# Two of eight weighted one-hots made by GpSimd, eight U blocks fewer ahead of the expert loop, and later loads of G: a hybrid encoder layer on one core

## The chip, the cores and the metric

The kernel runs on one core of a Trainium2 chip. The metric is the device time of one execution in microseconds (us). Three runs of the kernel before gave 1571.31, 1573.11 and 1576.31; their median is 1573.11 us. The profile is of one further execution. The core has a matrix engine (TensorE, PE in the profile; PEld are its weight loads), VectorE (DVE), ScalarE (ACT), GpSimd (POOL) and SyncE (SP), each with a queue of its own that it works off in order, and 16 DMA engines that all queues share.

## The reference

One encoder layer over 512 tokens of width 1024, all in float32: a layer norm; a projection; neighbourhood attention and latent attention; an output projection; a layer norm; then the expert layer (PEER) with a gated embedding term; a last layer norm. The change touches only the expert layer:

```python
q = (xb @ w_q).reshape(128, 8, 256)                       # 8 heads
s1, s2 = q[..., :128] @ sub_keys[0].T, q[..., 128:] @ sub_keys[1].T
v1, i1 = top_k(s1, 16);  v2, i2 = top_k(s2, 16)
cv, ci = top_k(all 256 sums v1 + v2, 16)                  # 16 experts a head
e1, e2 = i1[ci // 16], i2[ci % 16]                        # expert number = 128 * e1 + e2
g = softmax(cv)
hpre = einsum('td,ted->te', xb, u_table[128 * e1 + e2])   # 16384 rows of U, V
out  = einsum('te,ted->td', g * gelu(hpre), v_table[128 * e1 + e2])
```

Each token so uses 128 of 16384 rows of U and as many of V, with the weights g.

## The kernel before

**Two ways to reach the rows.** The tokens stand in four chunks of 128. For chunk 0 the kernel fetches each token's rows of U and V by indirect DMA from GpSimd (gathers). For the other 384 tokens it goes through all 128 blocks of 128 experts: for each block it multiplies with the block's V and weights that are zero where a token did not pick an expert. These weights are G (block by block, from DRAM) times the activation `ge` = gelu(U x). For 96 of the 384 tokens (the "own rows", `own_rows`, L1025) the products with U are also made from gathered rows, and only 288 tokens (N_U) go through U blocks.

**Ahead of the loop.** Under a schedule written out by hand, five strands run together:

- `route` (L863), on VectorE: the top 16 and the picks of one chunk.
- `build_g` (L956): makes G for one chunk in 16 passes of eight tokens (OT). A pass makes eight one-hots of e1 (`oh_i`: the first few by one VectorE operation at L997, the rest by ScalarE at L1001 and L1002) and eight one-hots of e2, weighted with g (`oh_j`: eight VectorE operations at L1010). TensorE multiplies them pairwise (`products`, L976), ScalarE copies the result out (L987), and every second pass ScalarE's queue writes 1 MB of G to DRAM (L989). The tiles have two buffers, so a pass takes the buffers of the pass before the last one.
- `own_rows`: 96 gathers of 512 KB by GpSimd (L1045) into four buffers (`whi`, `wlo`), each used by one VectorE operation (L1047).
- The gate's products (L104 to L106) and their cuts.
- U blocks ahead (`lead_block`, L1082): LEAD = 73 blocks are loaded (L1067, three buffers) and multiplied uncut in float32 (L1092), eight products each; the result is activated by ScalarE (L1074). The first SPILL = 56 results go to DRAM (L1076) and are read back in the loop (L1371); the rest stay in SBUF, in LEAD - SPILL + 1 buffers.

What TensorE does between two VectorE steps is set by a planner: each strand yields the VectorE time that it has issued, `run_pe` (L947) adds it times PACE to `due`, and takes U products and gate products off their list until `due` is used up. `run` (L1196) does the same for the own rows with a share (OWN = 0.98): for each microsecond of other VectorE work it issues that share of own-row work. The order of the builds is: route chunk 1, then route and build chunks 2 and 3 among the own rows, route chunk 0, and last build chunk 1 (L1236 to L1239), with five of eight `oh_i` from VectorE instead of two.

**The passage.** After the last build GpSimd's queue holds seven gathers for chunk 0 (L1276), the first load of G (L1250, in two parts), and further gathers; the last U blocks ahead, the first loads of V and the first blocks' cuts come beside them (L1323 to L1341).

**The loop** (L1345) takes one block of V a step. VectorE multiplies G with `ge` (L1376), ScalarE and VectorE cut V and the weights into two parts of float32r (`split`, L86), TensorE makes 18 products of 512 columns into six sums (`acc`, `mm3`). As long as blocks of U are left (n + 1 + LEAD < 128), the step also makes one of them (`expert_in`, L770): a load, a cut and 24 products of 288 columns. The gathers of chunk 0 (L1276, L1291) and their VectorE operations (L1282, L1293) are spread over the steps, half as many in steps without a U block (LATE). G is loaded for eight steps at a time into two buffers, in the middle of the group before (L1348), from SP's queue; V's loads (L1260) and the read back `ge` stand in the same queue.

Of the kernel before, what the change touches and what calls it, by code (L numbers as in the profile page):

```python
# [15 lines left out]
OP = mybir.AluOpType  # L16
# [17 lines left out]
N_U = N_D - N_S  # L34
GT = 16
GB = 8
LEAD = 73
SPILL = 56
FIRST = 8
PACE = 1.1  # L40
AHEAD = 14.0
LAG = 6.0
PRE = 14
OWN = 0.98
OWN_LATE = 10.0
LATE = 0.5
OT = 8
OV = 5
OV_OWN = 2
NEG = -1e30  # L50
# [15 lines left out]
def tile_encoder_layer(ctx: ExitStack, tc: tile.TileContext, A: dict, out: bass.AP):  # L66
    nc = tc.nc
# [689 lines left out]
    NGC, NDC = N_G // 128, N_D // 128  # L757
# [32 lines left out]
    iota = rt.tile([128, 128], F32, name="iota")  # L790
# [41 lines left out]
    first = []  # L832
# [120 lines left out]
        if due < -1e6:  # L953
            due = 0.0

    def build_g(c, e1, e2, gw, first):  # L956


        nonlocal due
        ps = ps_tile("tr")  # L960
        for i, x in enumerate((e1, e2, gw)):
            nc.tensor.transpose(ps[:, i * 128:(i + 1) * 128], x, ident)
        due -= 0.35
        yield None
        eT = bt.tile([128, 3, 128], F32, name="eT")
        nc.vector.tensor_copy(eT, ps[:, 0:384].rearrange("p (a b) -> p a b", b=128))
        yield 0.6
        ne = bt.tile([128, 128], F32, name="ne")
        nc.scalar.mul(ne, ps[:, 0:128], -1.0)

        def products(q, oi, oj):
            out = []
            for r in range(OT // 4):
                ps = ps_tile("tr")
                for i in range(4):
                    nc.tensor.matmul(ps[:, i * 128:(i + 1) * 128], oj[:, 4 * r + i, :], oi[:, 4 * r + i, :],  # L976
                                     start=True, stop=True)
                out.append(ps)
            return out

        def leave(q, sums):
            nonlocal stage
            if q * OT % GT == 0:
                stage = bt.tile([128, 128, GT], F32, name="g_st")
            for r, ps in enumerate(sums):
                x = OT * q % GT + 4 * r
                nc.scalar.copy(stage[:, :, x:x + 4], ps.rearrange("p (t i) -> p i t", t=4))  # L987
            if (q + 1) * OT % GT == 0:
                nc.scalar.dma_start(g_dram[(c - NGC) * (128 // GT) + q * OT // GT], stage.rearrange("p i t -> p (i t)"))  # L989

        stage = None
        ahead = None
        for q in range(128 // OT):
            t0 = OT * q

            oi = bt.tile([128, OT, 128], F32, name="oh_i")
            nc.vector.tensor_tensor(oi[:, 0:first], iota.unsqueeze(1).to_broadcast([128, first, 128]),  # L997
                                    eT[:, 0, t0:t0 + first].unsqueeze(2).to_broadcast([128, first, 128]),
                                    op=OP.is_equal)
            for i in range(first, OT):  # L1000
                nc.scalar.activation(oi[:, i], iota, AF.Abs, bias=ne[:, t0 + i:t0 + i + 1])  # L1001
            nc.scalar.activation(oi[:, first:OT], oi[:, first:OT], AF.Relu, bias=1.0, scale=-1.0)  # L1002
            if ahead:
                sums = products(*ahead)
                due -= 1.8
            yield 0.15 * first

            oj = bt.tile([128, OT, 128], F32, name="oh_j")
            for i in range(OT):
                nc.vector.tensor_scalar(oj[:, i], iota, eT[:, 1, t0 + i:t0 + i + 1], eT[:, 2, t0 + i:t0 + i + 1],  # L1010
                                        op0=OP.is_equal, op1=OP.mult)
                if i == OT // 2 - 1:
                    yield 0.257 * OT / 2
            if ahead:
                leave(ahead[0], sums)
            ahead = (q, oi, oj)
            yield 0.257 * OT / 2
        sums = products(*ahead)
        due -= 1.8
        yield 0.3  # L1020
        leave(ahead[0], sums)
# [60 lines left out]
    def lead_block():  # L1082


        while len(raws) < 3 and loaded < LEAD:
            load_u()
# [109 lines left out]
    def run(steps, share=0.0, n=2):  # L1196

        nonlocal own_due
        for amount in steps:
            if amount is None:  # L1200
                for _ in range(n if own else 0):
                    run_pe(next(own, 0.0))
                continue
            run_pe(amount)
            own_due += amount * share
            while own and own_due > 0:
                x = next(own, None)
                if x is None or not x:
                    own_due = -1e9
                    break  # L1210
                run_pe(x)
                own_due -= x

    with tc.manual_schedule(engines={nc.vector.engine, nc.scalar.engine, nc.tensor.engine, nc.sync.engine,
                                     nc.gpsimd.engine}):
        for _ in range(3):
            load_u()
        held = []
        run(route(NGC, held))
        own = own_rows(*held)  # L1220
        run_pe(next(own))
        own_due = -OWN_LATE
        for c in range(NGC + 1, 4):
            res = []
            run(route(c, res), OWN)
            run(build_g(c, *res, OV_OWN), OWN)
        lead0 = route(0, [])
        for _ in range(14):
            run([next(lead0)], OWN)
        own_due = 1e9  # L1230
        run([0.0], 1.0)
        for _ in own:
            pass
        own = None
        run_pe(LAG)
        build = build_g(NGC, *held, OV)  # L1236
        next(build)
        run(lead0)
        run(build)  # L1239
        pb.close()  # L1240
# [82 lines left out]
    with tc.manual_schedule(engines={nc.vector.engine, nc.scalar.engine, nc.tensor.engine, nc.sync.engine,  # L1323
# [3 lines left out]
        gt_next = load_g(0, nc.gpsimd, ((128 // GT, NTG), (0, 128 // GT)))  # L1327
# [15 lines left out]
    with tc.manual_schedule(engines={nc.vector.engine, nc.sync.engine}):  # L1343
        expert_in(LEAD)
        for n, i in enumerate(order):  # L1345
            if n % GB == 0:
                gt = gt_next
            if n % GB == GB // 2 and n + GB // 2 < 128:  # L1348
                gt_next = load_g(n + GB // 2)
            raw = v_next[n] if n < 3 else load_v(n)  # L1350
            if n in v_cut:
                vh, vl = v_cut[n]
                ah = pP.tile([128, N_D], F32R, name="a_hi")
                al = pP.tile([128, N_D], F32R, name="a_lo")
            elif n in (124, 125):
                vh = wst.tile([128, D], F32R, name="whi")
                vl = wst.tile([128, D], F32R, name="wlo")
                a2 = wst.tile([128, 2, N_D], F32R, name="raw", bufs=3)
                ah, al = a2[:, 0], a2[:, 1]
            else:  # L1360
                if in_wst(n):
                    vh = wst.tile([128, D], F32R, name="whi")
                    vl = wst.tile([128, D], F32R, name="wlo")
                else:
                    vh = pP.tile([128, D], F32R, name="v_hi")
                    vl = pP.tile([128, D], F32R, name="v_lo")
                ah = pP.tile([128, N_D], F32R, name="a_hi")
                al = pP.tile([128, N_D], F32R, name="a_lo")
            if 0 <= n + GE_AHEAD - (128 - SPILL) < SPILL:
                ge = pB.tile([128, N_U], F32, name="ge", bufs=LEAD - SPILL + 1)  # L1370
                nc.sync.dma_start(ge, ge_dram[order[n + GE_AHEAD]])  # L1371
                ge_t[order[n + GE_AHEAD]] = ge
            ge = ge_t.pop(i)
            a = gt[:, :, n % GB, :]
            dn = gt[:, N_S // GT:, n % GB, :]
            nc.vector.tensor_tensor(dn, dn, ge.rearrange("p (g t) -> p g t", t=GT), op=OP.mult)  # L1376
            if n not in v_cut:
                split(vh, vl, raw)
            split(ah.rearrange("p (g t) -> p g t", t=GT), al.rearrange("p (g t) -> p g t", t=GT), a)
            late.append((n, ah, al, vh, vl))  # L1380
            if n < 124:
                for c in range(NDC):
                    expert_out(late[0], c)
                late = []
            if n + 1 + LEAD < 128:
                expert_in(n + 1 + LEAD)
            if n >= NO_GATHER:
                spent += 1 if n + LEAD < 128 else LATE
            upto = min(len(steps), PRE + math.ceil((len(steps) - PRE) * spent / (128 - (1 - LATE) * LEAD - 3 - NO_GATHER)))
            for f in steps[done:upto]:  # L1390
                f()
            done = upto
        for c in range(NDC):
            for hf in range(2):
                for x in late:
                    expert_out(x, c, (hf,))
# [101 lines left out]
```

## Time and profile before

| | us |
|---|---|
| median of three runs | 1573.11 |
| the profiled execution | 1577.96 |
| its span, first to last instruction | 1576.2 |
| TensorE busy in the span | 1536.5 |
| VectorE busy | 1311.2 |
| ScalarE busy | 691.5 |
| GpSimd busy | 490.2 |
| granted TensorE clock, mean | 0.994 |

The busy time of an engine is the time in which at least one of its instructions runs. TensorE's records overlap, so what one product costs is read from the distance of two starts, as the chain of waits gives it. A line number can be that of a helper: L104 to L106 are the products of every cut matrix, L89 and L90 every cut. A row of the chain is: start, length, engine, tile, line, count. A row of the timeline is: start, length, engine, line, operation, tiles, shapes, count, and in brackets the idle time before it and what ended it. A row by tile or line is: shortest, median and longest duration in ns, first and last start.

### The profile page before, as it was taken

To read this page: it belongs to the slowest core of one execution; us is meant where nothing else is said; L and a number is where in the kernel's file an instruction comes from. 1 tells how busy PE (TensorE), PEld (TensorE's weight loads), DVE (VectorE), ACT (ScalarE), POOL (GpSimd) and SP (SyncE) were. 2 spreads that over 40 slices of the span, in tenths; PEclk is the share of its full clock that TensorE was granted. 3 is DMA by queue.
4 is the path that set the end of the run, shared out by engine and by line. 5 is a ranking of instruction groups with operands and counts; after the bars stand their busy time and mean duration, and the time that the engine had idled before them with its cause. 6 is when DMAs were issued, how large, how long until landed. Compare 5 with 4: busy or idle time off the path is not lost.

```text
span 1576.2 us, 23358 instructions
## 1 busy us (share of the span) xinstructions
PE 1536.5 (97%) x7963; PEld 1277.3 (81%) x7963; DVE 1311.2 (83%) x2989; ACT 691.5 (44%) x1269; POOL 490.2 (31%) x496
## 2 busy tenths in 40 slices
PE   9999999999999999999998999999999999999997
PEld 5788777788878887878786889889899888787885
DVE  7376785679899999789894899889889889799997
ACT  3365675333224672565562343434444333333333
POOL 1013110010024233432104455545555534344410
PEclk9999999999999999999999999999999999999999
DMA  6333230152369999999669999999999999999972
GB/s 224 97 112 95 76 121 28 52 153 81 106 211 347 348 377 346 362 381 373 237 237 387 376 383 378 387 376 349 376 374 338 363 368 381 387 372 387 384 285 80
DMA packets 204571, 437.21 MB, mean 277 GB/s; under 512 B 16770, under 2 KB 110370, under 8 KB 201380
## 3 DMA queue, kind: packets, MB, share of 16 engines
q1 hardware_dynamic: 138592, 210.27, 38.6%
q0 software_dynamic: 53984, 191.97, 32.7%
q10 hardware_dynamic: 11876, 33.49, 5.5%
q8 instruction: 63, 1.03, 0.3%
q14 instruction: 56, 0.46, 0.1%
HBM read 394.54 MB, written 37.62 MB: 274 GB/s over the span
## 4 chain that ended last, share of the span: by engine, by line
PE 76%; DVE 9%; DMA 7%; issue 5%; POOL 2%; ACT 1%; SPq 0%; POOLq 0%; DVEq 0%; ACTq 0%
PE acc L104 10%; PE acc L106 10%; PE acc L105 10%; PE mm L1092 5%; PE tr L976 4%; PE hp L104 4%; PE hp L105 4%; PE hp L106 4%; PE pj L104 3%; PE mm L104 3%; PE pj L105 3%; PE pj L106 3%; PE mm L106 3%; PE mm L105 3%; PE hp L1092 2%
## 5 line engine op out<-in xcount | busy, mean ns | idle before, releaser
L1291 POOL DMA_INDIRECT gat<-in_v_rows_dram,i_sel x128 | 169.6, 1325 | 204.0 <-DVE base L1293 179.4
L1276 POOL DMA_INDIRECT gat<-in_u_rows_dram,i_sel x128 | 168.9, 1320 | 181.4 <-DVE scr L1282 124.4
L104 PE MATMUL acc<-v_hi,a_hi 128*128 128x512 f32 x552 | 216.3, 392 | 3.8 <-ACT a_hi L89 3.8
L106 PE MATMUL acc<-v_hi,a_lo 128*128 128x512 f32 x552 | 216.5, 393 | 0.0
L105 PE MATMUL acc<-v_lo,a_hi 128*128 128x512 f32 x552 | 215.6, 391 | 0.0
L90 DVE TENSOR_TENSOR wlo<-raw,whi 128x1024 fp32r<-128x1024 f32 (+3 forms) x134 | 157.0, 1172 | 67.4 <-ACT whi L89 56.0
L89 ACT CAST whi<-raw 128x1024 fp32r<-128x1024 f32 (+3 forms) x134 | 135.1, 1009 | 140.0 <-PE mm L105 40.4
L89 ACT CAST v_hi<-v_raw 128x1024 fp32r<-128x1024 f32 x92 | 96.6, 1050 | 203.0 <-issue 126.7
L1293 DVE SCALAR_TENSOR_TENSOR base<-gat,hdot,base 128x1024 f32<-128x1024 f32 x128 | 163.9, 1280 | 1.7
L1282 DVE SCALAR_TENSOR_TENSOR scr<-gat,h 128x1024 f32<-128x1024 f32 x128 | 156.6, 1223 | 2.9
L1092 PE MATMUL mm<-whole,raw 128*128 128x288 f32 x624 | 157.7, 406 | 0.5 <-ACT ge L1074 0.4
L1092 PE MATMUL hp<-whole,raw 128*128 128x288 f32 x544 | 138.8, 410 | 5.3 <-DMA raw<-in_uT_dram 5.3
L89 ACT CAST a_hi<-gt 128x384 fp32r<-128x384 f32 x126 | 64.6, 513 | 180.3 <-DVE gt L1376 122.1
L1092 PEld LDWEIGHTS mm<-whole,raw 128*128 128x128 f32 x624 | 115.8, 190 | 30.7 <-issue 1.3
L90 DVE TENSOR_TENSOR v_lo<-v_raw,v_hi 128x1024 fp32r<-128x1024 f32 x92 | 112.6, 1223 | 24.1 <-issue 12.0
L1092 PEld LDWEIGHTS hp<-whole,raw 128*128 128x128 f32 x544 | 103.3, 192 | 33.6 <-issue 4.2
L104 PE MATMUL hp<-hTh,whi 128*128 128x288 f32 x440 | 130.2, 296 | 0.0
L106 PE MATMUL hp<-hTh,wlo 128*128 128x288 f32 x440 | 129.9, 295 | 0.0
L105 PE MATMUL hp<-hTl,whi 128*128 128x288 f32 x440 | 129.8, 295 | 0.0
L104 PEld LDWEIGHTS acc<-v_hi,a_hi 128*128 128x128 f32 x552 | 104.0, 189 | 24.6 <-ACT a_hi L89 4.4
L106 PEld LDWEIGHTS acc<-v_hi,a_lo 128*128 128x128 f32 x552 | 103.8, 188 | 23.6 <-DVE a_lo L90 0.9
L105 PEld LDWEIGHTS acc<-v_lo,a_hi 128*128 128x128 f32 x552 | 104.1, 189 | 20.8 <-issue 0.2
(375 smaller groups left out, 3383.7 us busy)
## 6 DMA issues: line engine op xcount, KB each, us to landing
raw<-in_uT_dram SPq DMA_DIRECT2D x128, 512.0 KB
v_raw<-in_v_rows_dram SPq DMA_DIRECT2D x94, 512.0 KB
g_dram<-g_st ACTq DMA_DIRECT2D x24, 1024.0 KB
gt<-g_dram SPq DMA_DIRECT2D x15, 1536.0 KB
raw<-in_v_rows_dram SPq DMA_DIRECT2D x34, 512.0 KB
raw<-in_w_in_dram SPq DMA_DIRECT2D x16, 512.0 KB
raw<-in_w_q_dram SPq DMA_DIRECT2D x16, 512.0 KB
ge_dram<-ge ACTq DMA_DIRECT2D x56, 144.0 KB
```

The costliest lines, as they stand in the source:

```text
L89: nc.scalar.copy(hi, src)
L90: nc.vector.tensor_tensor(lo, src, r32(hi), op=OP.subtract)
L104: nc.tensor.matmul(ps, a[0], b[0], start=start, stop=False)
L105: nc.tensor.matmul(ps, a[0], b[1], start=False, stop=False)
L106: nc.tensor.matmul(ps, a[1], b[0], start=False, stop=stop)
L976: nc.tensor.matmul(ps[:, i * 128:(i + 1) * 128], oj[:, 4 * r + i, :], oi[:, 4 * r + i, :], start=True, stop=True)
L1092: nc.tensor.matmul(ps[:, :N_U], raw[:, k], whole[:, k, :], start=(k == 0), stop=(k == 7))
L1276: nc.gpsimd.indirect_dma_start(out=u[:], out_offset=None, in_=u_rows, in_offset=bass.IndirectOffsetOnAxis(ap=i_sel[:, c, k:k + 1], axis=0))
L1282: nc.vector.scalar_tensor_tensor(scr, u, 1.0, h[c], op0=OP.mult, op1=OP.mult, accum_out=hdot[:, c, k:k + 1])
L1291: nc.gpsimd.indirect_dma_start(out=u[:], out_offset=None, in_=v_rows, in_offset=bass.IndirectOffsetOnAxis(ap=i_sel[:, c, k:k + 1], axis=0))
L1293: nc.vector.scalar_tensor_tensor(base[c], u, hdot[:, c, k:k + 1], base[c], op0=OP.mult, op1=OP.add)
```

## The change

In a build, the last `pooled` of a pass's eight `oh_j` are made by GpSimd instead of VectorE, with the same operation: two in chunks 2 and 3, four in the last build (chunk 1). They are issued ahead of VectorE's. The planner's costs follow VectorE's smaller share, and the own rows' share in the builds becomes 1.25 (OWN_B), so that each pass keeps its two own rows. LEAD becomes 65 and SPILL 48: eight blocks of U less ahead of the loop, eight more in it, eight results less written and read back; 17 stay in SBUF as before. In the loop, a group of G that is loaded at a step without a U block is loaded at the group's seventh step instead of its fifth, so two loads of V come ahead of it in SP's queue.

```diff
-LEAD = 73
-SPILL = 56
+LEAD = 65
+SPILL = 48
...
+OWN_B = 1.25
...
+OP_OWN = 2
+OP_LAST = 4
...
-    def build_g(c, e1, e2, gw, first):
+    def build_g(c, e1, e2, gw, first, pooled):
...
-            for i in range(OT):
-                nc.vector.tensor_scalar(oj[:, i], iota, eT[:, 1, t0 + i:t0 + i + 1], eT[:, 2, t0 + i:t0 + i + 1],
-                                        op0=OP.is_equal, op1=OP.mult)
-                if i == OT // 2 - 1:
-                    yield 0.257 * OT / 2
+            mine = OT - pooled
+            for i in list(range(mine, OT)) + list(range(mine)):
+                engine = nc.vector if i < mine else nc.gpsimd
+                engine.tensor_scalar(oj[:, i], iota, eT[:, 1, t0 + i:t0 + i + 1], eT[:, 2, t0 + i:t0 + i + 1],
+                                     op0=OP.is_equal, op1=OP.mult)
+                if i == mine // 2 - 1:
+                    yield 0.257 * (mine // 2)
...
-            yield 0.257 * OT / 2
+            yield 0.257 * (mine - mine // 2)
...
-            run(build_g(c, *res, OV_OWN), OWN)
+            run(build_g(c, *res, OV_OWN, OP_OWN), OWN_B)
...
-        build = build_g(NGC, *held, OV)
+        build = build_g(NGC, *held, OV, OP_LAST)
...
-            if n % GB == GB // 2 and n + GB // 2 < 128:
-                gt_next = load_g(n + GB // 2)
+            if n % GB == (GB // 2 if n < 128 - LEAD + 4 else GB - 2) and n // GB < 128 // GB - 1:
+                gt_next = load_g(n // GB * GB + GB)
```

## The prediction

> **What bounds the kernel now.** First the page: its span, TensorE's share, and the DMA rate slice by slice.
>
> ```profile
> span 1576.2 us, 23358 instructions
> PE 1536.5 (97%) x7963; PEld 1277.3 (81%) x7963; DVE 1311.2 (83%) x2989; ACT 691.5 (44%) x1269; POOL 490.2 (31%) x496
> ...
> GB/s 224 97 112 95 76 121 28 52 153 81 106 211 347 348 377 346 362 381 373 237 237 387 376 383 378 387 376 349 376 374 338 363 368 381 387 372 387 384 285 80
> ...
> raw<-in_uT_dram SPq DMA_DIRECT2D x128, 512.0 KB
> ...
> ge_dram<-ge ACTq DMA_DIRECT2D x56, 144.0 KB
> ```
>
> A share over the whole span hides which wait ends last, so next the busy time of each engine by stage (columns: PE, PEld, DVE, ACT, POOL busy with counts, clock, DMA share, GB/s). The stages: build of chunk 2, build of chunk 3, the last build (chunk 1), the passage to the loop, the loop's steps with a U block, its steps without.
>
> ```profile
> 491.70:590.50 98.80, 98.16 (x539) 82.83 (x538) 91.27 (x235) 71.44 (x169) 31.54 (x33) 1.00 0.99 365
> 646.20:736.00 89.80, 87.03 (x487) 72.92 (x486) 76.57 (x210) 65.07 (x159) 31.00 (x33) 1.00 0.99 380
> 766.30:823.00 56.70, 54.12 (x359) 47.91 (x359) 51.56 (x154) 41.95 (x104) 5.86 (x7) 1.00 0.70 260
> 823.00:857.60 34.60, 27.32 (x114) 20.95 (x112) 13.12 (x21) 7.39 (x12) 15.85 (x15) 0.95 0.98 362
> 857.60:1261.00 403.40, 401.63 (x2286) 359.95 (x2287) 361.01 (x490) 158.25 (x220) 212.27 (x154) 1.00 1.00 371
> 1261.00:1566.30 305.30, 303.83 (x1315) 245.65 (x1314) 267.75 (x341) 109.65 (x151) 105.95 (x84) 1.00 0.92 337
> ...
> 491.70:743.90 252.20, 248.29 (x1291) 204.82 (x1290) 226.16 (x618) 148.82 (x352) 84.22 (x84) 1.00 0.99 369
> ```
>
> The loop is TensorE alone: 401.6 of 403.4 us and 303.8 of 305.3. The two builds that hold the own rows (all gathers of `own_rows` are used by 743.9) are full on two sides: TensorE at 97 to 99% and the DMA engines at 0.99. VectorE stands at 85 to 92%. In the last build the DMA engines have room (0.70).
>
> Third, the chain of waits, for what one piece of TensorE work takes: a U block ahead of the loop (16 records), a pass's eight products, a U block inside the loop (24 rows from 869.50 to 872.70), and a step's output products (18 rows from there).
>
> ```profile
> 549.46 3.88 PE hp L1092 x16
> 553.35 1.78 PE tr L976 x16
> ...
> 869.50 0.14 PE hp L104
> ...
> 872.57 0.13 PE hp L106
> 872.70 0.23 PE acc L104
> ...
> 876.59 0.23 PE acc L106
> ```
>
> So a U block costs 3.88 us ahead and 3.20 us in the loop.
>
> **The change part by part.** *Eight U blocks move from ahead of the loop into it.* The activation of each block in the loop dates the steps:
>
> ```profile
> L777 ACT ACTIVATE ge<-hp x55: 395/404/408, 860.0 to 1260.6; 128x288 f32<-128x288 f32 x55
> ```
>
> 54 steps in 400.6 us are 7.42 us a step; the 74 steps after it take 305.3, 4.13 each. Eight steps change from 4.13 to 7.42: +26 us. Bounds: 8 x 3.20 = 25.6 and 8 x 3.29 = 26.3; TensorE hides nothing here, because it is the bound. Each block also brings one more split; VectorE has room (361 of 403). DMA: 8 x 0.52 MB more U, less 8 x 0.15 MB of `ge` read back, on 403.4 x 371 + 305.3 x 337 = 253 MB that now have 26 us longer: covered. The gathers stay the same in number, spread thinner.
>
> Ahead of the loop the same blocks free 8 x 3.88 = 31 us of TensorE. If all of that left the time, the change would win 5 us. The question is what is late next, and it differs by stage. By the order of the two programs, 2.2 of the eight are gone by the start of chunk 3's build and 4.6 by the start of the last one; own rows keep their places, two a pass (so the new share 1.25 costs nothing: it only makes up for shorter passes).
>
> *Own part, 491.7 to 743.9.* TensorE loses 4.6 x 3.88 = 18 us, VectorE 64 one-hots. Their price, and a pass of the last build:
>
> ```profile
> 783.98 0.82 DVE L997 TENSOR_TENSOR oh_i<-iota,eT 128x640 f32<-128x640 f32 x1
> 784.72 2.15 DVE L1010 TENSOR_SCALAR oh_j<-iota,eT 128x128 f32<-128x128 f32 x8
> 786.77 0.83 DVE L997 TENSOR_TENSOR oh_i<-iota,eT 128x640 f32<-128x640 f32 x1
> ```
>
> Eight in 2.15, 0.27 us each: 64 are 17 us. But DMA loses only 4.6 x 0.67 = 3.1 MB of 252.2 x 369 = 93 MB: 8.4 us at the same rate. At the best slice's 387 GB/s the remaining 90 MB would take 233 us, 20 less; that is the other end. What speaks against it is GpSimd's queue. It runs in order, and now two one-hots stand behind every two gathers. A one-hot of pass q waits for the products of pass q-2, whose buffer it takes; the gathers behind it wait too, and VectorE waits for those. How long a gather takes, and that VectorE already waits:
>
> ```profile
> 682.83 10.18 DMA whi<-in_u_rows_dram,s_sel
> ```
>
> ```profile
> DVE whi L1047 <- DMA whi<-in_u_rows_dram,s_sel: 14.0, 10, 2.1
> ```
>
> ```profile
> 676.63 1.22 DVE L1047 SCALAR_TENSOR_TENSOR whi<-whi,h_s 128x1024 f32<-128x1024 f32 x1 [1.28 <-DMA whi<-in_u_rows_dram,s_sel]
> ...
> 677.78 0.42 DVE L997 TENSOR_TENSOR oh_i<-iota,eT 128x256 f32<-128x256 f32 x1
> 678.12 1.11 DVE L1010 TENSOR_SCALAR oh_j<-iota,eT 128x128 f32<-128x128 f32 x4
> ```
>
> A pass is 89.8/16 = 5.6 us. Counted from the start of pass q-1, the products of q-2 end at about 1.8, two one-hots at 2.4, and the gather is out at 3.3; VectorE wants it at 5.6 + 2.3 (own row 1.15, `oh_i` 0.34, three `oh_j` 0.8). That leaves 4.6 us. Before, a gather went out when the own row four places earlier was used: four half passes of 2.8, less 1.2 for that row and 1.2 for the issue, left about 9, and landing took 10.2 with four in flight. With two in flight, 4.6 us at 380 GB/s move 1.75 MB, and the gather with the other traffic's share (0.52 + 0.89) fits just so. So the queue eats between 0 and some 0.5 us a pass (16 us in 32 passes). The own part comes out between -20 and +8; I take -4, half the fall that the bytes allow, because both ends need one of two full resources to give.
>
> *Last build.* VectorE loses 4 x 0.27 a pass, and of U's products between the passes 51 become 27 in the order, so TensorE loses 24/8 x 3.88 = 12 us of 57. Before, the products of 13 passes stand between these rows, 12 intervals of 3.08 us:
>
> ```profile
> 778.81 1.78 PE tr L976 x16
> ...
> 815.77 1.78 PE tr L976 x16
> ```
>
> ```profile
> 780.00:820.00 40.00, 40.00 (x273) 36.12 (x272) 37.84 (x119) 31.93 (x79) 0.00 (x0) 1.00 0.62 232
> ```
>
> ScalarE is next: 31.9 of 40 us, 2.46 a pass. GpSimd's one-hot does not stand in the trace; its nearest rows:
>
> ```profile
> 313.00 0.23 POOL L789 IOTA iota_i<- 128x128 int32 x1 [88.68 <-PE mm L105]
> ...
> 316.67 6.19 POOL L813 TENSOR_TENSOR whole<-hTh,hTl 128x288 f32<-128x288 f32 x8 [1.77 <-DVE hTl L90]
> ```
>
> Between 0.23 (writes 128 columns, reads none) and 6.19/8 = 0.77 (reads two inputs of 288). I take 0.3, near the row of the same length. Four are 1.2 us, hidden behind ScalarE; at 0.77 they are 3.1 and nothing is won. So 0 to -10 us over 16 passes; I take -6.
> The Trainium skill's "GPSIMD Engine Reference", section "Elementwise — side-by-side cycle accounting", gives 1.03 cycles an element for a body of at most two operations; by that a one-hot would be an estimated 0.11 us and a dispatch, and the sum would be the same.
>
> *Passage to the loop.* Today GpSimd issues seven gathers in the last build's free DMA time, then stands waiting for G:
>
> ```profile
> 765.55 0.94 POOL L1276 DMA_INDIRECT gat<-in_u_rows_dram,i_sel  x1 [30.82 <-DVE gws L1053]
> ...
> 773.04 0.94 POOL L1276 DMA_INDIRECT gat<-in_u_rows_dram,i_sel  x1 [0.30 <-issue]
> 823.48 1.25 POOL L1250 DMA_DIRECT2D gt<-g_dram  x1 [49.50 <-PE tr L976]
> ```
>
> Now 64 one-hots stand ahead of them, so 7 x 0.52 = 3.7 MB come some 40 us later, into the stage where TensorE waits for U twice:
>
> ```profile
> 829.27 13.11 DMA raw<-in_uT_dram
> ...
> 848.35 7.43 DMA raw<-in_uT_dram
> ```
>
> At 387 GB/s that is 9.5 us if the cover is gone and 0 if it all fits before the last product; I take +4.
>
> *G's late loads.* The load waits on SP for VectorE's last use of the buffer; V's loads wait behind it.
>
> ```profile
> SPq L1250 <- DVE a_lo L90: 44.7, 7, 7.2
> ```
>
> Two V loads pass ahead of it now; G itself still goes out when its buffer comes free, eight steps ahead. TensorE idles 1.5 us in that stage, so at most that: -1.
>
> Sum: -4 -6 +4 = -6 ahead of the loop, +26 -1 in it: **+19 us**. The profiled execution took 1577.96 (span and 1.8 around it), 4.9 over the median 1573.11; laid on the median, **1592 us**.
>
> **The rivals.** *TensorE alone paces everything (faster).* Its 97 to 99% in the builds speak for it: then all 31 us leave, +26 -2 come back, -7: 1566. Against it: the own part would have to shrink by 18 us at a DMA rate that the trace shows only in its best slices, and the passage must not grow. It decides from 26 us saved ahead of the loop.
> *DMA gives its best rate (a little slower or equal).* Own part -20, the rest as above: -22 + 25 = +3, 1576. For it: the loop holds 371 GB/s over 400 us.
> *GpSimd's queue starves the own rows.* Half a microsecond to one a pass, 16 to 32 us over -8: lead +6 to +22, net +31 to +47, 1604 to 1620. For it: the 4.6 us above; against: fewer gathers in flight land sooner.
> *The one-hots only change place.* Both engines lengthen beside each other:
>
> ```profile
> L1010 DVE TENSOR_SCALAR oh_j<-iota,eT x384: 327/343/559, 494.8 to 816.9; 128x128 f32<-128x128 f32 x192
> ```
>
> ```profile
> L1045 POOL DMA_INDIRECT whi<-in_u_rows_dram,s_sel x48: 939/944/1687, 453.9 to 731.3; - x48
> ```
>
> If they excluded each other, a pass of the last build would be 0.74 + 4 x 0.27 + 4 x 0.3 = 3.0 us, nothing won: +25, 1598; at 0.77 it is 4.9, +29 more: 1627.
> The Trainium skill's "SBUF — State Buffer", section "Who interferes with whom", says just this: a VectorE operation in a two-port mode, or with two SBUF inputs, and a reading GpSimd operation block each other whole. The maxima above agree with it; no run yet shows two such streams.
>
> **How the numbers follow.** Forecast (1585 to 1604) 0.46; TensorE alone 0.18; DMA at its best 0.16; GpSimd's queue 0.15; excluded one-hots beyond 1604 0.05. A measurement here can tell about 0.3%, 4.7 us: faster is below 1568.4, the first rival, 0.18; same takes 0.12 of the DMA rival; slower is the rest, 0.70. The range reaches from 1565, the first rival's time, to 1612, the middle of the queue rival's; some 0.15 lies outside.
>
> **What would show it.** Right: loop steps of 7.4 us, 63 of them; TensorE idle in the builds with DMA still at 0.97 or more; the last build's passes at 2.5 to 2.8 us with ScalarE full; gathers of `gat` issued after the last one-hot. Wrong: the builds at over 385 GB/s and TensorE full (then faster); VectorE's waits for the `whi` rows well above 14.0 us, GpSimd idle before its one-hots (then slower); one-hots over 0.6 us on GpSimd, or `oh_j` on VectorE over 0.4 in the mean.

## The result, and the profile after

The changed kernel takes 1658.33 us, the median of four runs from 1653.32 to 1662.07, beside 1572.21 us for the kernel before: a ratio of 1.0525, 95% interval 1.0488 to 1.0561 (the ratios in this document are not exactly the quotients of the medians). So it is slower, and by some 86 us instead of the 19 that were forecast. The profiled execution took 1662.07 us.

First the stages, in the columns of the prediction's table (busy time of PE, PEld, DVE, ACT, POOL with counts, clock, DMA share, GB/s): build of chunk 2, build of chunk 3, last build, passage, loop with U blocks, loop without; then the part with the own rows as a whole.

```profile
492.10:613.00 120.90, 101.74 (x517) 84.33 (x516) 82.89 (x199) 70.21 (x166) 78.26 (x67) 0.90 0.80 286
672.90:779.90 107.00, 85.51 (x442) 72.12 (x441) 69.56 (x177) 64.78 (x156) 75.94 (x66) 0.89 0.83 297
814.60:881.20 66.60, 52.98 (x311) 42.39 (x311) 30.16 (x81) 40.98 (x99) 64.85 (x68) 1.00 0.37 150
881.20:923.00 41.80, 26.60 (x108) 20.37 (x108) 18.98 (x29) 7.06 (x12) 19.06 (x19) 0.84 1.02 382
923.00:1384.00 461.00, 461.00 (x2638) 414.04 (x2637) 405.66 (x538) 182.07 (x255) 237.29 (x168) 1.00 0.99 365
1384.00:1650.60 266.60, 266.60 (x1158) 216.53 (x1156) 234.80 (x304) 95.23 (x132) 85.89 (x69) 1.00 0.90 326
```

```profile
492.10:792.40 300.30, 253.75 (x1225) 207.99 (x1224) 213.19 (x554) 148.05 (x347) 173.36 (x149) 0.91 0.84 301
```

The own part, from the first copy of `eT` to the end of the last own row, went from 252.2 to 300.3 us (+48.1), the last build from 56.7 to 66.6 (+9.9), the passage from 34.6 to 41.8 (+7.2), the loop from 708.9 to 727.6 (+18.7). With 0.2 us elsewhere that is the 84.1 us between the two spans, 1576.2 and 1660.3. (The prediction's row for the build of chunk 2 ends at 590.5, 4 us before that build's last product; like for like, its 98.8 us are 103.1, beside 120.9 now.) In the own part nothing is full any more: TensorE fell from 98% to 84%, DMA from 0.99 to 0.84, VectorE from 90% to 71%, GpSimd stands at 58%. No resource is the bound by itself; they wait for each other in turn. The granted TensorE clock, 1.00 before, is 0.91 here; what that costs, no run shows by itself. In the last build one engine is full, and it is GpSimd: 64.85 of 66.60.

Next, who waits, from 480 to 900 us (engine, line, waited for; sum, times, longest).

```profile
DVE wlo L1052 <- DMA wlo<-in_u_rows_dram,s_sel: 53.9, 23, 6.1
POOL oh_j L1015 <- PE tr L979: 49.1, 16, 16.5
...
DVE whi L1052 <- DMA whi<-in_u_rows_dram,s_sel: 30.1, 15, 4.4
PE tr L979 <- DVE oh_j L1015: 29.6, 13, 5.2
```

The same view of the kernel before has for the other pair of buffers:

```profile
DVE wlo L1047 <- DMA wlo<-in_u_rows_dram,s_sel: 6.7, 7, 1.6
```

VectorE's waits for the own rows were 14.0 and 6.7 us and are 30.1 and 53.9. GpSimd waits 49.1 us for products before its one-hots, and TensorE waits for VectorE's one-hots. What a one-hot takes, in ns (shortest, median, longest):

```profile
L1015 DVE TENSOR_SCALAR oh_j<-iota,eT x256: 331/342/684, 495.4 to 874.4; 128x128 f32<-128x128 f32 x128
L1015 POOL TENSOR_SCALAR oh_j<-iota,eT x128: 783/835/2436, 492.7 to 876.1; 128x128 f32<-128x128 f32 x128
```

On VectorE it costs what it did; on GpSimd never less than 783 ns, where the prediction took 300.

### The profile page after: what moved, and what is told of

Read it like the earlier page. It is cut to its first block, busy times and chain, and to the rows that moved or that the text cites. A ratio compares the mean times of both kernels' runs of the same rounds, so it can differ in the third digit from the quotient of the medians.

```text
span 1660.3 us, 23579 instructions
## 1 busy us (share of the span) xinstructions
PE 1561.2 (94%) x8027; PEld 1298.5 (78%) x8027; DVE 1294.2 (78%) x2869; ACT 698.7 (42%) x1277; POOL 643.4 (39%) x624
## 3 DMA queue, kind: packets, MB, share of 16 engines
q8 instruction: 63, 1.03, 0.2%
## 4 chain that ended last, share of the span: by engine, by line
PE 72%; DMA 9%; DVE 8%; POOL 5%; issue 4%; ACT 1%; SPq 0%; POOLq 0%; DVEq 0%; ACTq 0%
PE acc L107 10%; PE acc L109 10%; PE acc L108 10%; DMA wlo<-in_u_rows_dram,s_sel 5%; POOL oh_j L1015 5%; PE hp L107 4%; PE hp L109 4%; PE hp L108 4%; PE hp L1097 3%; PE pj L107 3%; PE mm L107 3%; PE pj L109 3%; PE pj L108 3%; PE mm L109 3%; PE mm L108 3%
## 5 line engine op out<-in xcount | busy, mean ns | idle before, releaser
L107 PE MATMUL acc<-v_hi,a_hi 128*128 128x512 f32 x576 | 224.8, 391 | 0.0
L109 PE MATMUL acc<-v_hi,a_lo 128*128 128x512 f32 x576 | 224.8, 391 | 0.0
L108 PE MATMUL acc<-v_lo,a_hi 128*128 128x512 f32 x576 | 224.2, 390 | 0.0
L92 ACT CAST whi<-raw 128x1024 fp32r<-128x1024 f32 (+3 forms) x138 | 139.2, 1010 | 132.4 <-PE mm L108 40.4
L1015 POOL TENSOR_SCALAR oh_j<-iota,eT 128x128 f32<-128x128 f32 x128 | 129.9, 1023 | 95.7 <-PE tr L979 49.1
L979 PE MATMUL tr<-oh_i,oh_j 128*128 128x128 f32 x768 | 116.4, 298 | 43.5 <-DVE oh_j L1015 29.6
L979 PEld LDWEIGHTS tr<-oh_i,oh_j 128*128 128x128 f32 x768 | 104.7, 203 | 58.8 <-DVE oh_j L1015 26.4
L107 PE MATMUL hp<-hTh,whi 128*128 128x288 f32 x504 | 149.0, 296 | 1.7 <-ACT ge L1079 1.7
L109 PE MATMUL hp<-hTh,wlo 128*128 128x288 f32 x504 | 148.8, 295 | 0.4 <-DVE wlo L93 0.4
L108 PE MATMUL hp<-hTl,whi 128*128 128x288 f32 x504 | 148.7, 295 | 0.0
L93 DVE TENSOR_TENSOR v_lo<-v_raw,v_hi 128x1024 fp32r<-128x1024 f32 x96 | 117.5, 1224 | 14.9 <-ACT v_hi L92 13.3
L1097 PE MATMUL mm<-whole,raw 128*128 128x288 f32 x480 | 126.7, 421 | 2.4 <-DMA raw<-in_uT_dram 2.4
```

The costliest lines, as they stand in the source:

```text
L92: nc.scalar.copy(hi, src)
L93: nc.vector.tensor_tensor(lo, src, r32(hi), op=OP.subtract)
L107: nc.tensor.matmul(ps, a[0], b[0], start=start, stop=False)
L108: nc.tensor.matmul(ps, a[0], b[1], start=False, stop=False)
L109: nc.tensor.matmul(ps, a[1], b[0], start=False, stop=stop)
L1015: engine.tensor_scalar(oj[:, i], iota, eT[:, 1, t0 + i:t0 + i + 1], eT[:, 2, t0 + i:t0 + i + 1], op0=OP.is_equal, op1=OP.mult)
```

## The experiments

**Theories.** *A, the order:* on GpSimd's queue a one-hot that waits for the products of the pass before the last holds up the gathers behind it; VectorE then waits for the own rows. *B, the price:* a one-hot takes 0.8 to 1.1 us of GpSimd, and GpSimd becomes the bound. *The rival:* the eight missing U blocks, not the one-hots, cost the time ahead of the loop.

All runs by stage, from the starts in the profiled execution of each: own part here from the first copy of `eT` to the third (the measure that the expectations use), last build from there to its last product, passage to the first `acc` product, loop to the last.

| kernel | median us | ratio to before (95%) | own part | last build | passage | loop |
|---|---|---|---|---|---|---|
| before | 1571.36 to 1575.69 | 1 | 274.6 | 56.6 | 34.7 | 708.9 |
| changed | 1658.33 | 1.0525 (1.0488–1.0561) | 322.5 | 66.6 | 41.8 | 727.6 |
| U blocks and G | 1593.02 | 1.0126 (1.0086–1.0167) | 271.2 | 59.4 | 16.7 | 743.7 |
| one-hots alone | 1667.05 | 1.0610 (1.0559–1.0660) | 320.3 | 66.6 | 71.6 | 704.5 |
| zeros | 1611.46 | 1.0241 (1.0185–1.0296) | 294.6 | 49.9 | 41.0 | 727.5 |
| gathers ahead | 1628.72 | 1.0350 (1.0296–1.0405) | 287.0 | 66.5 | 42.3 | 727.7 |
| zeros, gathers ahead | 1582.64 | 1.0072 (1.0054–1.0090) | 262.7 | 49.9 | 40.4 | 727.5 |
| one-hots in own builds only | 1643.29 | 1.0484 (1.0445–1.0523) | 312.1 | 55.2 | 26.8 | 737.1 |
| one-hots in last build only | 1610.48 | 1.0250 (1.0233–1.0268) | 272.6 | 66.9 | 26.0 | 746.5 |
| G late alone | 1569.68 | 0.9954 (0.9934–0.9973) | 273.4 | 56.4 | 34.6 | 704.3 |
| before, gathers ahead, G late | 1568.47 | 0.9962 (0.9945–0.9979) | 271.1 | 54.2 | 35.6 | 703.8 |
| one one-hot a pass | 1571.15 | 0.9969 (0.9953–0.9984) | 269.2 | 49.4 | 49.4 | 702.2 |
| 81 blocks ahead, G late | 1573.88 | 1.0001 (0.9984–1.0019) | 270.3 | 55.0 | 63.7 | 681.3 |

### The two halves of the change

```diff
-OWN_B = 1.25
-OP_OWN = 2
-OP_LAST = 4
+OWN_B = 0.98
+OP_OWN = 0
+OP_LAST = 0
```

> The eight U blocks in the loop and the late loads of G, without one-hots on GpSimd. Theory B (a one-hot is dear on GpSimd, 0.8 to 1.0 us, and GpSimd becomes the bound) and theory A (GpSimd's in-order queue sends the own rows' gathers late) both lay the loss ahead of the loop on the one-hots: the builds of chunks 2 and 3 come back to 99 and 90 us or less (117 and 107 in the changed kernel), the last build to 57 or less, VectorE's waits for the own rows to about 20 us, and the time is that of before plus the loop's 19 to 26: 1588 to 1598 us. The rival (the missing U blocks themselves cost time ahead of the loop, since TensorE stands idle in the passes and its clock falls): the builds stay over 105 us and the time over 1630. If TensorE alone had paced the builds before, they would fall by 18 us and the time would be below 1580.

Measured: 1593.02 us. The builds are back: from the copy of `eT` to the last product, those of chunks 2 and 3 take 103 and 87 us, where the kernel before takes 103 and 90. The rival falls. The last build missed its figure: it takes 59.4 us instead of at most 57, and TensorE stands there for 7.7 us, for ScalarE's copies and for the cut of a U block, where it stood 2.6 before. And the table says more: the eight blocks brought the loop's start forward by 19 us (838.7 after 857.6), and then gave most of it back. The passage of this run, and its chain of waits:

```profile
822.00:838.70 16.70, 0.01 (x2) 0.01 (x1) 9.79 (x16) 3.18 (x4) 8.87 (x8) 0.59 0.96 330
```

```profile
819.95 2.07 PE tr L979 x16
822.04 0.59 ACT g_st L990
822.65 5.80 DMA g_dram<-g_st
...
829.01 8.45 DMA gt<-g_dram
...
838.69 0.79 PE acc L107
...
841.49 31.03 DMA v_raw<-in_v_rows_dram
```

TensorE does nothing for 16.7 us: the last piece of G must be written out (5.8) and read back (8.45). After the idle stretch, in which the granted clock is 0.59, the first products start 0.43 us apart instead of 0.23. In the loop's first four steps TensorE stands twice more, for 3.9 and 6.1 us, the second time until the load of V that stands last above has landed. In the kernel before, U products filled most of the passage (27.3 of 34.6 us). So the blocks were worth their place as cover too, not only as work: 8 x 3.88 = 31 us of TensorE left the stages ahead, 19 showed, and the loop lost 16 to waits and slow products, where the changed kernel's loop loses none.

```diff
-LEAD = 65
-SPILL = 48
+LEAD = 73
+SPILL = 56
...
-            if n % GB == (GB // 2 if n < 128 - LEAD + 4 else GB - 2) and n // GB < 128 // GB - 1:
+            if n % GB == GB // 2 and n // GB < 128 // GB - 1:
```

> One-hots on GpSimd alone: 73 blocks of U ahead, G's loads where they were. By theories A and B the stages ahead of the loop lose what they lost in the changed kernel, 60 to 75 us, and the loop is as before: 1630 to 1650 us. The rival (the loss comes from the missing U blocks): within 10 us of before, 1565 to 1583. A mixed case (U's products fill the gaps that the one-hots leave): 1600 to 1625.

Measured: 1667.05 us, 17 over the range. The own part and the last build are those of the changed kernel, so the one-hots alone make the loss there; the passage is 71.6 us, 30 more than in the changed kernel, because the eight more blocks (8 x 3.88 = 31) are all left over for it: the planner hands them out by VectorE's work, and VectorE has less of it. The whole change is not slower than this, so beside the one-hots the move of the U blocks cost nothing: in the changed kernel, too, U blocks are left over for the passage (TensorE works in 26.6 of its 41.8 us), and its wait for G is not bare as in the run before.

### Order or price

Zeros instead of the one-hots, the same queue and the same waits for buffers:

```diff
+                if i >= mine:
+                    nc.gpsimd.memset(oj[:, i], 0.0)
+                else:
+                    nc.vector.tensor_scalar(oj[:, i], iota, ...)
```

> The changed kernel, but GpSimd writes zeros into the same tiles instead of the weighted one-hots (those tokens' share of G is left out). Order on GpSimd's queue and the waits for the buffers stay; the price falls and the two inputs are not read. Theory A (the order in the queue): the own rows wait as much as in the changed kernel, 85 us, and the time stays at 1645 to 1665. Theory B (the price): VectorE's waits for the own rows fall to under 35 us, the last build to a pass of under 3.1 us, and the time to 1580 to 1600.

Measured: 1611.46 us (two runs), between the two. GpSimd's instruction now takes 0.2 us, and it still waits:

```profile
L1015 POOL MEMSET oh_j<- x128: 194/204/314, 486.7 to 827.0; 128x128 f32 x128
```

```profile
POOL oh_j L1015 <- PE tr L979: 110.0, 39, 16.5
...
DVE wlo L1054 <- DMA wlo<-in_u_rows_dram,s_sel: 40.6, 17, 6.3
```

GpSimd's wait for products rose from 49.1 to 110.0 us: what it no longer works it waits, and the gathers wait with it. VectorE's waits for the own rows, 14.4 us for `whi` beside the 40.6, add up to 55: less than the changed kernel's 84, more than the 35 that theory B allows. So the price is the larger part, 47 us, and the order alone is worth the 23 us by which this own part exceeds that without one-hots. On this run's chain of waits stand late gathers:

```profile
698.37 9.03 DMA wlo<-in_u_rows_dram,s_sel
...
714.05 8.73 DMA wlo<-in_u_rows_dram,s_sel
...
727.25 9.51 DMA wlo<-in_u_rows_dram,s_sel
```

The other way round, the real one-hots, but each gather issued three places ahead of its use (`fetch` issues the gather of one row):

```diff
+        rows = [fetch(k) for k in range(3)]
...
+                if k + 3 < N_S:
+                    rows.append(fetch(k + 3))
+                u = rows.pop(0)
```

> The changed kernel with each gather of an own row issued three places earlier in GpSimd's program than its use, so that it stands ahead of the one-hots that held it up. Theory A: the builds of chunks 2 and 3 lose most of their 35 us of extra time, and the total comes to 1605 to 1630. Theory B: GpSimd still has two one-hots and two gathers a pass to do, some 5 us with their stretching; the gain is at most 15 us and the total stays above 1640.

Measured: 1628.72 us (two runs), as theory A had it: the own part loses 35 of the 51 us that it has over the one without one-hots, the time 30. How the two theories interlock is read from two chains. The changed kernel's, in the build of chunk 3:

```profile
690.76 9.37 DMA wlo<-in_u_rows_dram,s_sel
...
702.16 0.70 DVE whi L1052
...
703.30 0.78 DVE oh_j L1015 x3
...
705.20 2.91 POOL oh_j L1015 x2
708.12 0.16 issue
708.28 5.61 DMA whi<-in_u_rows_dram,s_sel
```

It is a ring: a gather lands, VectorE uses the row and only then makes its one-hots, TensorE's products with these free a buffer (GpSimd waits for them 2.58 us here), GpSimd makes its two in 2.91 us, and the next gather can go out. With the gathers ahead the chain of waits is GpSimd's own work:

```profile
684.24 1.07 POOL whi L1049
...
686.10 1.87 POOL oh_j L1015 x2
...
688.14 1.00 POOL wlo L1049
...
690.44 1.70 POOL oh_j L1015 x2
```

Two one-hots and two gathers are what is left, and GpSimd is the bound.

The zeros and the gathers three places ahead, both edits at once:

> Both suspects taken away at once: zeros of the same size in place of GpSimd's one-hots (those tokens' share of G is left out) and the own rows' gathers three places earlier in GpSimd's program. If A and B together are the whole loss beside the U blocks, the own part falls to 265 to 275 us (294 with zeros alone, 287 with the gathers ahead alone) and the total to 1580 to 1595. If something else holds it (VectorE or TensorE waiting for GpSimd's tile at each pass), the own part stays over 282 us and the total over 1598.

Measured: 1582.64 us, own part 262.7, even a little under the range. Set against the 1593.0 of the run without any GpSimd one-hots, the changed kernel loses 65.3 us, the zeros leave 18.4 of it, the gathers ahead 35.7, both together -10.4. The price brings 46.9, the order 29.6, the two together 75.7: they add up, and there is no third cause of this size. (The zeros read no inputs, so the price here holds what VectorE adds to a one-hot by holding it up.) What stays is the gain that the change was to bring ahead of the loop.

```profile
490.20:729.10 238.90, 229.48 (x1209) 190.86 (x1208) 211.16 (x554) 146.60 (x348) 100.79 (x155) 0.99 0.98 375
752.90:802.80 49.90, 44.66 (x311) 39.21 (x311) 30.39 (x82) 39.09 (x98) 14.76 (x62) 1.00 0.52 196
```

The first row is the own part in the prediction's measure: 238.9 against 252.2, at 375 GB/s instead of 369. The second is the last build: 49.9 against 56.7, now with ScalarE at 39.1; from 757.75 to 784.26, where a pass takes 2.65 us, ScalarE is busy for 24.2 of 26.5.

### Where the loss lies

```diff
-OP_LAST = 4
+OP_LAST = 0
```

> U blocks and G's loads as in the changed kernel; GpSimd makes its two one-hots only in the builds of chunks 2 and 3, none in the last build. The own part (from the first copy of eT to the third) keeps the changed kernel's 322 us against 271 with no one-hots on GpSimd, so by theories A and B alike the total is 1593 plus 30 to 51: 1623 to 1644 us; the low end if the later start of the loop hides the 16 us for which the loop waited without any one-hots. The rival (the four one-hots of the last build are the main loss): under 1610.

Measured: 1643.29 us (1633.26 to 1654.15, the widest of all).

```diff
-OWN_B = 1.25
-OP_OWN = 2
+OWN_B = 0.98
+OP_OWN = 0
```

> U blocks and G's loads as in the changed kernel; GpSimd makes four one-hots a pass in the last build alone, none before. Theory B (0.96 us each, four are 3.85 us a pass): the last build takes 64 to 68 us against 59 without, products 3.85 us apart; the total is 1593 plus 0 to 25, 1593 to 1618, the low end if the lengthening lies in the time for which the loop waited anyway. Theory A has nothing to say here, since no own gathers stand behind these one-hots; if they only queued and did not pace, the last build would be at 50 to 57 us and the total at 1585 to 1593.

Measured: 1610.48 us, last build 66.9. Over the 1593.0 these are 50 and 17 us, together 67, and the whole change has 65. Three quarters lie in the own part, as near as the wide scatter of the first of the two runs lets it be told. In the last build theory B stands alone, and the changed kernel's timeline shows it: VectorE's one-hots, four a pass, begin every 3.85 us after 2 us of idle time, while GpSimd runs without a gap.

```profile
839.78 0.82 DVE L1000 TENSOR_TENSOR oh_i<-iota,eT 128x640 f32<-128x640 f32 x1 [2.00 <-issue]
840.53 1.11 DVE L1015 TENSOR_SCALAR oh_j<-iota,eT 128x128 f32<-128x128 f32 x4
843.63 0.82 DVE L1000 TENSOR_TENSOR oh_i<-iota,eT 128x640 f32<-128x640 f32 x1 [2.00 <-ACT g_st L990]
```

```profile
838.36 18.39 POOL L1015 TENSOR_SCALAR oh_j<-iota,eT 128x128 f32<-128x128 f32 x19
```

19 in 18.39 us are 0.97 each, four 3.87; a pass before took 3.08.

### The price by itself

48 instructions on GpSimd ahead of the routing, on a tile filled with ones:

```diff
+    probe = rt.tile([128, 2, 256], F32, name="probe")
+    nc.gpsimd.memset(probe, 1.0)
+    px, pz = probe[:, 0], probe[:, 1]
+    for _ in range(8):
+        nc.gpsimd.tensor_scalar(pz[:, 0:128], px[:, 0:128], px[:, 0:1], px[:, 1:2], op0=OP.is_equal, op1=OP.mult)
...
```

> The kernel before with 48 added instructions on GpSimd ahead of the routing, eight of each form: the weighted one-hot's form with 128, 256 and 32 columns, the same with two constants, a product of two tiles of 128 columns, and a copy of 128. The prediction's price (0.3 us for the weighted one-hot) would show at the form's shortest here; theory B says 0.78 us or more with nothing beside it, and the longer forms tell the fixed part from the part by column: 0.78 us at 128 columns by the column alone would be 1.5 at 256 and 0.2 at 32; by the fixed part alone 0.78 at all three.

```profile
L796 POOL TENSOR_SCALAR probe<-probe x8: 787/792/1051, 312.2 to 319.6; 128x128 f32<-128x128 f32 x8
L798 POOL TENSOR_SCALAR probe<-probe x8: 1212/1217/1402, 320.5 to 332.8; 128x256 f32<-128x256 f32 x8
L800 POOL TENSOR_SCALAR probe<-probe x8: 466/470/1324, 334.8 to 342.5; 128x32 f32<-128x32 f32 x8
L802 POOL TENSOR_SCALAR probe<-probe x8: 640/642/1145, 343.1 to 348.1; 128x128 f32<-128x128 f32 x8
L804 POOL TENSOR_TENSOR probe<-probe x8: 455/461/463, 349.4 to 353.1; 128x128 f32<-128x128 f32 x8
L806 POOL COPY probe<-probe x8: 293/293/1344, 353.7 to 357.2; 128x128 f32<-128x128 f32 x8
```

The one-hot's form takes 0.79 us by itself. Between 32 and 256 columns it grows by (1217 - 470) / 224 = 3.3 ns a column, so about 0.36 us are there at any width. Constants in place of the two columns of values save 0.15 us, a product of two tiles takes 0.46, a copy 0.29.

### What pays

> The kernel before with the late loads of G alone. The prediction has 1 us of gain, at most the 1.5 us that TensorE stood idle in that stage: 1568 to 1574 us beside 1571 to 1573. A rival (a late load delays the splits of G's values and TensorE waits for them): 1578 or more.

The edit is the change's last hunk alone. Measured: 0.9954 (0.9934 to 0.9973), 4 to 10 us of gain. The loop shrinks from 708.9 to 704.3. SP's waits over the loop show the place, first in the kernel before:

```profile
SPq L1250 <- DVE a_lo L90: 50.8, 8, 7.2
```

With G late the loads of G wait for this:

```profile
SPq L1250 <- DVE base L1293: 1.2, 1, 1.2
...
SPq L1250 <- DVE a_lo L90: 0.8, 2, 0.6
```

SP no longer stands in front of a buffer of G with V's loads behind it. (It does not wait less in all: its waits for `a_lo` in front of V's loads, L1260, rise from 14.6 to 47.6 us.) Of the gain the two profiles show 2 us in the stage that the edit touches, the steps without a U block (305.3 and 303.3 us); the rest lies in stages that it leaves alone. The runs of the kernel before, made beside these, scatter more (1566.57 to 1584.30, 35 runs) than those with G late (1565.48 to 1571.40, 12 runs), and why stays open, and with it whether the whole of the gain is the edit's.

> The kernel before with G's late loads and the own rows' gathers three places earlier, no one-hots on GpSimd, 73 blocks ahead. If GpSimd's order already cost time before (VectorE waited 21 us for the own rows), the own part falls from 275 us towards 263, and the time to 1558 to 1568. If TensorE is the bound of that part, as its 97 to 99% say, there are 4 us at most: 1567 to 1573, no change that can be told.

Measured: 0.9962, beside 0.9954 without the gathers ahead: no change that can be told. Where no one-hot stands between them, the gathers' order costs nothing that can be told.

> A version that the prices allow: one one-hot a pass on GpSimd (0.8 to 1.1 us, which fits beside two gathers of 1.2 in a pass of 5.6, and in a pass of 3.1 of the last build), the gathers three places ahead, G late, 73 blocks ahead. VectorE loses 0.27 us a pass. If VectorE and the gathers are the bound ahead of the loop: 5 to 12 us less than before, 1560 to 1568. If TensorE is: 1567 to 1575, the same as without the one-hots. If GpSimd's one-hots stretch VectorE's work by as much as they take from it: 1575 to 1585.

Measured: 0.9969 (0.9953 to 0.9984), no better than G late alone. The last build falls to 49.4 us as wished, and the passage takes it back, 49.4 instead of 34.6: TensorE's U products are only moved there. And GpSimd's single one-hot is dearer than one of several:

```profile
L1015 POOL TENSOR_SCALAR oh_j<-iota,eT x48: 803/1572/2731, 491.4 to 799.4; 128x128 f32<-128x128 f32 x48
```

> The opposite dose: 81 blocks of U ahead, with G's late loads, no one-hots on GpSimd. In the loop 8 steps fall from 7.4 to 4.1 us: 26 us less. Ahead of it TensorE gets 31 us of work; if it is the bound there, all but the idle time that takes some of it (7 us in the passage, 3 in the last build, 4 before) comes on top, 17 to 31: 1563 to 1578 us. If G's way through memory is what sets the passage, as without the eight blocks, the extra work lies beside it and the time falls below 1560.

Measured: 1.0001, and 0.0047 above G late alone. The loop loses 23 us (704.3 to 681.3), the passage gains 29: ahead of the loop TensorE has nothing free for more blocks.

So of the change's three edits only the late loads of G pay: about 0.4 to 0.5%, with or without the gathers ahead.

## Why the prediction was wrong

Its direction and its largest single term were right; its size was not, because of one price and one wait.

- **The loop, +26: right.** The changed loop has no wait of TensorE left and takes 727.6 us; before it took 708.9, of which 6.4 were stalls (distances of over 0.3 us between the starts of successive products, less the 0.23 of a product). 727.6 - 702.5 = 25.1, beside 25.6 to 26.3. That the stalls would go as well (the loop so pays only 18.7) was not foreseen.
- **G's late loads, -1: near in its stage, small against the time.** The stage gives 2 us where the bound was the 1.5 us that TensorE stood idle; the timed gain of the edit alone, 4 to 10 us, is larger than its stage explains.
- **The price of GpSimd's one-hot: this is the step that failed first, and it cost the most.** "I take 0.3, near the row of the same length." The row (IOTA) shares only the length; it reads nothing and computes nothing from a tile. The other row, 0.77, does both. Measured: 0.79 where nothing holds it up, 0.97 in the last build. Nor was 0.77 an upper end: in the own builds the mean is over 1 us, the longest 2.44.
- **Last build, -6: wrong by that price alone.** It became +9.9. With the price at 0.2 it is 49.9, which is -6.8: the step itself, ScalarE next in line, held (a pass in 2.65 us, within the forecast 2.5 to 2.8).
- **Own part, -4: wrong by the price, and by a second step, the gathers' landing.** It became +48.1. The count "two one-hots at 2.4, gather out at 3.3" has 0.6 us for two; they take 1.6 alone and 2.9 in the chain above. But the zeros, at 0.2 us each, are cheaper than the 0.3 of the prediction, and with them the own part still takes 269.2 us in the prediction's measure: +17, outside the -20 to +8. It is 22 us over that of the run without GpSimd's one-hots (247.1), 0.7 us for each of 32 passes, where the sum had 0 to 0.5. What failed there is "the gather with the other traffic's share fits just so": the sum had a gather landing within 4.6 us with two in flight, and the ones shown on the two chains take 5.6 to 9.5; how much of that other traffic makes was not measured. The queue rival had the right mechanism and place, and with a cheap instruction also the size (1611.46 us, in its 1604 to 1620). With the real price the own part lies 53 us over 247.1, 1.7 a pass. Without both causes it is 238.9: -13.3, inside the -20 to +8 and nearer to its fast end. The rows of the zeros and of the run without GpSimd's one-hots:

```profile
490.40:759.60 269.20, 241.10 (x1203) 196.78 (x1202) 209.20 (x554) 147.51 (x346) 109.80 (x154) 0.96 0.91 333
```

```profile
491.40:738.50 247.10, 245.48 (x1283) 203.04 (x1282) 226.24 (x618) 149.07 (x352) 84.00 (x84) 1.00 0.99 373
```

- **Passage, +4: within its bounds.** It is +7.2; how much of that the seven late gathers make, no run shows. But the prediction did not see that U products cover G's way through memory there, which is what a smaller number of blocks runs into first; alone, the move of the U blocks came out at 1593.0, close to the forecast 1592 for the whole change. That is luck: the reason is another than the forecast's.
- **The chances.** The starving queue (0.15) and one-hots at 0.77 (0.05) were held to be separate cases, with times of up to 1620 and 1627. Neither excludes the other, and the dear one-hot makes the queue worse, so they came together; a range for them would have had to add 32 and 29 us and end near 1650. The prediction's own signs for this way of being wrong all came: VectorE's waits for `whi` at 30.1 us, GpSimd idle before its one-hots, one-hots over 0.6 us. The rivals on the fast side needed the cheap one-hot as well: with it, zeros and gathers ahead give 1582.64 us, and even that is slower than the kernel before. (The first of them stands at 1566 in its sum and at 1565 in the range; nothing hangs on it.)

## What to carry to other kernels

Before work goes to another engine, find its price there in a row of the same form, one that reads what it reads and computes what it computes; where the trace has none, carry the dearest row through every step that uses the price, not only through one. An engine whose queue issues gathers should not get work that waits for another engine between them, unless the gathers are issued well ahead; and two suspicions that can both be true at once make a case of their own, in which their costs add. What a transfer's way through memory takes is seen only when the work that covers it is gone, so ask of each piece of work that is moved away what waits behind it.

## What the runs showed of the hardware that was not expected

- An operation with a column of values for each of its two scalars costs 0.79 us on GpSimd for 128 columns, against 0.46 for a product of two whole tiles and 0.29 for a copy: the form sets the price as much as the length does. VectorE has one every 0.27. The Trainium skill's "GPSIMD Engine Reference", section "Elementwise — side-by-side cycle accounting", gives 1.03 cycles an element for bodies of at most two operations, the source of the prediction's side estimate of 0.11 us and a dispatch, which would be an estimated 0.9 ns a column; here a column costs 3.3 ns and 0.36 us come on top, so the page's figure does not hold for this form, and the measurement decides.
- GpSimd's one-hot is held up by VectorE's operations with two tiles as inputs, for their whole length. With one one-hot a pass, it starts in the last build together with VectorE's `oh_i`, and takes 1.57 us, which is 0.79 and nearly all of the 0.83; in the changed kernel one of four falls on it and takes 1.46, the other three, beside VectorE's one-hots, 0.79, so that a pass's four take some 3.85. The timelines of GpSimd and VectorE in the run with one one-hot a pass:

```profile
777.38 1.57 POOL L1015 TENSOR_SCALAR oh_j<-iota,eT 128x128 f32<-128x128 f32 x1 [1.18 <-PE tr L979]
```

```profile
777.37 0.83 DVE L1000 TENSOR_TENSOR oh_i<-iota,eT 128x640 f32<-128x640 f32 x1
778.12 1.88 DVE L1015 TENSOR_SCALAR oh_j<-iota,eT 128x128 f32<-128x128 f32 x7
```

  VectorE is not slowed there: 0.83 us and 0.27 a one-hot, as before. The Trainium skill's "SBUF — State Buffer", section "Who interferes with whom", states just this block, that of a reading GpSimd operation by a VectorE operation with two inputs in SBUF; these rows agree with it. In the own builds, where VectorE's own rows of 1.2 us are of that kind, the longest one-hot is 2.44 us.
- With enough U blocks to cover G's way, a U block costs nearly the same ahead of the loop as in it: from 73 to 81 the loop loses 23 us and starts 24 later (879.2 after 855.0), and the times stand at 0.9954 and 1.0001 of the kernel before.
